# A transformer block on one core: three quarter products of the second MLP product split again into seven, weight sums made in DRAM by adding transfers

## The chip, the core and the metric

The program runs on one core of one Trainium2 chip. The metric is the device time of one execution in microseconds; lower is better. The kernel before was run three times: 1228.98, 1229.09 and 1229.5 us, median 1229.09 us. One more execution was recorded by the profiler and gives the trace that is read here. The engines are PE (TensorE: matmuls, with PEld for its weight loads), DVE (VectorE), ACT (ScalarE), POOL (GpSimd) and SP (SyncE, which issues most of the DMAs here; ACT and POOL issue DMAs from queues of their own).

## The reference

One layer of a hybrid encoder, 1024 tokens by 1024 channels, float32. What matters here is the order of the stages and the last two lines:

```python
h = rms(x, norm1_g[l]).astype(dt)
p = h @ w_in[l]
...
mix_a = mlstm_group(qk_m, ...)
mix_b = diff_attention_group(...)
mixed = jnp.concatenate([mix_a, mix_b], axis=-1).astype(dt)
x = x + (mixed @ w_out[l]).astype(dt)
u = rms(x, norm2_g[l]).astype(dt) @ w_ff1[l]
u = jnp.square(jax.nn.relu(u))
x = x + (u @ w_ff2[l]).astype(dt)
```

`w_ff1` is 1024 x 4096 and `w_ff2` 4096 x 1024. `mlstm_group` has 4 heads of 128 with a forward and a backward scan over 8 chunks of 128 tokens, `diff_attention_group` 4 heads over blocks of 128 queries. The last line, `u @ w_ff2`, is the second MLP product.

## The kernel before

The program goes through its stages one after the other: start and projections, mLSTM (about 134 to 340 us), attention (340 to 565), the output projection and the second norm (to 612), the first MLP product (612 to 917) and the second (917 to 1223).

**Precision.** Each float32 operand is cut into a high part (ACT, `cut_hi`, L1736) and a low part (DVE, `cut_lo`, L1739). A product of tiles is three matmuls into one PSUM bank: high by high, low by high, high by low (for the second MLP product lines L2152, L2153, L2154).

**Quarter products.** Both MLP products are done by the Strassen-Winograd scheme: the matrices are halved both ways, and seven products of halves, numbered 1 to 7, take the place of eight; sums of halves are made before, and sums of products after. The first MLP product writes, for each of the seven, the token side that the second needs to DRAM (`g_dram`, seven times eight tiles of 128 x 1024). Its last steps are the sums `sums1`, `sums2`, `sums3` of a pair of tiles and the stores of these.

**The second MLP product** (L2066 to L2240) has seven products in the order 1, 6, 2, 5, 7, 3, 4, each of 8 steps. A step (`z_step`, L2136) takes one tile of weights (`wa`: `wa0h`, `wa0l`, `wa1h`, `wa1l`) and one of tokens (`wb`, `we`: `wbh`, `wbl`, `weh`, `wel`), and has 24 matmuls of 128 x 128 weights by 128 x 512 tokens. Both kinds of cut tiles have two buffers, which the steps use by turns. The sums of weight halves are made by DVE on the raw weights: `za+zs` (L2115), `za-zd` (L2112), `zs+zd` (L2226), `zt+za` (L2116), eight of each. `finish` (L2183) recombines the products, on DVE, ACT and a little on POOL, with the residual, and stores the output. The last step's output tile is done in two halves of 256 columns, stored from ACT's and SP's queues (`last_out`, L2169).

**Order.** Instructions of each engine run in the order in which they stand in its program. That order comes from tables: `when(t, f, ...)` puts a piece of work at a planned time `t`, and the pieces are emitted in order of `t`. In the MLP the unit of `t` is half a step of the second product (2.725 us by the plan), and `T2` is where the second product begins. In the mLSTM stage a heap of the same kind is emptied while the projection's matmuls are emitted, with `clock` as its time. DMAs on SP's queue can also come out in another order than they were emitted, by what each waits for.

**The mLSTM stage** interleaves two streams on PE: projections (`pj_c`, `pva`) and the heads. For each head and each half `g` of the chunks, `load(g)` (L1102) loads two broadcast tiles of 512 KB, `e` from `m_dram` (decays) and `qs` from `sc_dram` (scales); head 0's are called e00, qs00, e01 and qs01 in what follows. `select` (L1116, POOL) masks `e`; `exps` (L219, ACT) exponentiates it; `scores` (L1177, DVE) multiplies it by the scores; `scaled` (L1181, DVE) multiplies `qs` by `q`; `sums` (L1194 and L1196, PE, tile `tot`) uses both. Then `divide`, `squares`, `unit` and `turned` (L1209, L180, L1224, L1230) normalise and turn the head's output; of these POOL has the tensor operations with `to` and `nd`. POOL also makes the low parts of the projection's weights (L1028: `w_c`, `w_va`). In the attention stage POOL has small operations, most of them on `sm` (L1435).

Of the kernel before, what the change touches and what calls it, by code (L numbers as in the profile page):

```python
# [10 lines left out]
F32 = mybir.dt.float32  # L11
# [129 lines left out]
def hybrid_block_kernel(ctx: ExitStack, tc: tile.TileContext, xT, xR, w_v, w_k, w_c, w_va, w_qg, w_o, w_1, w_2, vec, rel, outT):  # L141
# [20 lines left out]


# [1480 lines left out]

    gate_pieces()
# [138 lines left out]
    for j in range(4):  # L1784
# [147 lines left out]
    for c in range(N_PAIR):  # L1932
# [17 lines left out]
        when(e[4] + 0.28, sums1, c)  # L1950
        when(e[4] + 0.8, sums2, c)
        when(e[4] + 1.3 if c + 1 < N_FIRST else e[4] + 1.4, sums3, c)
        for d, i, f in ((0.9, 7, lambda c: gs1[c][:, 0]), (0.95, 5, lambda c: gs1[c][:, 1]),
                        (1.3, 6, lambda c: gs2[c][:, 0]), (1.9, 4, lambda c: gs2[c][:, 1])):
            when(e[4] + d, lambda c, i, f: store(i, c, f(c)), c, i, f)
# [139 lines left out]
    def load_za(j):
        za[j] = z_load(z_tile(f"za{j}", f"za{j}", pool="a"), j, 0, 0)

    def load_zs(j):
        zs[j] = z_load(z_tile(f"zs{j}", f"zs{j}"), j, 1, 0)

    def load_zd(j):
        zd[j] = z_load(z_tile(f"zd{j}", f"zd{j}"), j, 1, 1)

    def load_zt(i, j):
        zt[i, j] = z_load(z_tile(f"zt{i}_{j}", "zt", 3), j, 0, 1)

    def z_add(t, a, b):
        nc.vector.tensor_tensor(t[0], a[0], b[0], op=add)

    def z_seven(j):  # L2110
        zt[7, j] = z_tile(f"zt7_{j}", "zt", 3)
        nc.vector.tensor_tensor(zt[7, j], za[j], zd[j], op=sub)  # L2112

    zsum = {
        6: lambda j: nc.vector.tensor_tensor(za[j], za[j], zs[j], op=add),  # L2115
        3: lambda j: nc.vector.tensor_tensor(zt[3, j], zt[3, j], za[j], op=add),  # L2116
        7: z_seven,
    }
    zsrc = {1: lambda j: za[j], 6: lambda j: za[j], 5: lambda j: zs[j], 4: lambda j: zd[j]}
    graw = {}  # L2120

    def fetch(s):
        i, j = steps[s]
        graw[s] = ypool.tile([P, 2, HB], F32, tag=f"y0_{(s + 1) % 4}", name=f"g{i}_{j}")
        nc.sync.dma_start(graw[s], g_dram[i - 1][j].rearrange("c p t -> p c t"))

    def g_part(s):
        return (wb, we)[s % 2], graw[s]

    def z_part(s):  # L2130
        i, j = steps[s]
        return wa[s % 2], zsrc[i](j) if i in zsrc else zt[i, j]
# [194 lines left out]
```

## Time and profile before

| what | value |
|---|---|
| median of three runs | 1229.09 us |
| the profiled execution | 1229.11 us |
| its span (first to last instruction) | 1227.3 us |
| bytes moved by DMA | 218.04 MB, mean 178 GB/s |
| mLSTM, 134 to 340 us | the longest waits of PE: 0.8, 0.4, 0.3 and 0.3 us in all |
| the second product's first and last matmul | 917.5 and 1222.6 us |

The page is of one execution. "Busy" is the time in which an engine had an instruction; matmuls overlap, so the duration of one is longer than the distance between two. A row such as `PE tot L1194 <- DVE e L1177` says that PE, at the instruction that writes tile `tot`, waited for the instruction of L1177 that wrote `e` on DVE, and then for how long in all, how often, and the longest. In a timeline a bracket behind a row gives the idle time of the engine before it and what ended it. For a DMA, the engine's name with q means the queue that issued it, and the landing time is counted from the issue.

### The profile page before, as it was taken

What the parts mean: (1) busy time and instruction counts of PE and PEld (TensorE: products, weight loads), DVE (VectorE), ACT (ScalarE), POOL (GpSimd) and SP (SyncE); (2) the same over time, 40 slices, a digit from 0 to 9 for tenths busy, and PEclk for the clock granted to TensorE, in tenths of its full rate; (3) what the DMA queues carried; (4) which work ended last, traced back from release to release, by engine and by line L of the source; (5) the groups of instructions that cost most, each with busy time, mean ns of one, the idle gap of its engine ahead of it and who ended that gap; (6) DMA issues with size and microseconds to landing.
All of it is one profiled execution on the core that took longest, in us unless ns stands there. A gap on an engine that the chain in (4) does not pass through costs nothing.

```text
span 1227.3 us, 17165 instructions
## 1 busy us (share of the span) xinstructions
PE 1217.3 (99%) x6349; PEld 1020.7 (83%) x6349; DVE 848.1 (69%) x1202; ACT 651.2 (53%) x1158; POOL 242.7 (20%) x271
## 2 busy tenths in 40 slices
PE   9999999999999999999999999999999999999998
PEld 8889888888878878888887888888888888888886
DVE  7885668983277787674789886666754864558754
ACT  7785457676356676664465455454453433333332
POOL 2135323662344453321000000000000000014001
PEclk9999999999999999999999999999999999999999
DMA  9972665344364685517445764444369655435632
GB/s 284 237 242 105 214 137 135 98 139 131 129 199 161 209 281 171 169 61 267 161 152 195 252 217 128 155 160 140 137 217 377 214 188 188 145 121 164 222 115 92
DMA packets 106024, 218.04 MB, mean 178 GB/s; under 512 B 9424, under 2 KB 22224, under 8 KB 105936
## 3 DMA queue, kind: packets, MB, share of 16 engines
q1 hardware_dynamic: 84276, 168.27, 42.2%
q0 software_dynamic: 9856, 27.30, 7.6%
q10 hardware_dynamic: 11808, 21.37, 4.7%
q8 instruction: 50, 0.82, 0.3%
q14 instruction: 34, 0.28, 0.1%
HBM read 157.56 MB, written 58.30 MB: 176 GB/s over the span
## 4 chain that ended last, share of the span: by engine, by line
PE 86%; DVE 5%; DMA 4%; ACT 2%; issue 2%; POOL 1%; ACTq 0%; SPq 0%; DVEq 0%; POOLq 0%
PE z L2154 8%; PE z L2152 8%; PE z L2153 8%; PE m L1823 7%; PE m L1824 7%; PE m L1825 7%; PE pav L1426 4%; PE pva L1296 4%; PE pl L1386 3%; PE pv L435 3%; PE pvz L435 3%; PE pw L229 3%; PE pw L231 2%; PE pw L230 2%; PE pa L1414 2%
## 5 line engine op out<-in xcount | busy, mean ns | idle before, releaser
L2197 POOL TENSOR_TENSOR zx<-zx,res 128x512 f32<-128x512 f32 x4 | 8.7, 2179 | 491.6 <-DVE zx L2195 491.6
L1391 DVE CUSTOM_DVE_ANT_0 l<-pl,toe 128x1024 f32<-128x1024 f32 x64 | 76.3, 1221 | 17.0 <-PE pl L1386 15.9
L2154 PE MATMUL z<-wbh,wa0l 128*128 128x512 f32 x224 | 87.4, 390 | 0.1
L2153 PE MATMUL z<-wbl,wa0h 128*128 128x512 f32 x224 | 87.2, 389 | 0.0
L2154 PE MATMUL z<-weh,wa1l 128*128 128x512 f32 x224 | 87.2, 389 | 0.0
L2153 PE MATMUL z<-wel,wa1h 128*128 128x512 f32 x224 | 87.2, 389 | 0.0
L2152 PE MATMUL z<-wbh,wa0h 128*128 128x512 f32 x224 | 87.2, 389 | 0.0
L2152 PE MATMUL z<-weh,wa1h 128*128 128x512 f32 x224 | 87.2, 389 | 0.0
L1736 ACT ACTIVATE wbh<-g 128x1024 fp32r<-128x1024 f32 x28 | 29.7, 1061 | 90.2 <-PE z L2154 53.0
L1736 ACT ACTIVATE weh<-g 128x1024 fp32r<-128x1024 f32 x28 | 29.7, 1061 | 90.2 <-PE z L2154 53.4
L1739 DVE TENSOR_TENSOR wel<-g,weh 128x1024 fp32r<-128x1024 f32 x28 | 35.2, 1258 | 56.6 <-ACT weh L1736 56.6
L1872 ACT ACTIVATE sq<-sq 128x512 f32<-128x512 f32 x48 | 30.2, 630 | 82.3 <-DVE sq L1911 65.7
L1397 ACT ACTIVATE l<-l,sm 128x1024 f32<-128x1024 f32 x64 | 73.1, 1148 | 0.5 <-DVE sm L1391 0.5
L1739 DVE TENSOR_TENSOR wbl<-g,wbh 128x1024 fp32r<-128x1024 f32 x28 | 35.4, 1264 | 52.4 <-ACT wbh L1736 52.4
L1426 PEld LDWEIGHTS pav<-v,at 128*128 128x128 f32 x512 | 61.5, 192 | 3.4 <-issue 1.1
L1426 PE MATMUL pav<-v,at 128*128 128x128 f32 x512 | 62.7, 276 | 0.0
L1386 PE MATMUL pl<-kk,q 64*128 64x512 f32 x384 | 55.6, 410 | 1.1 <-DVE sm L1391 1.0
L229 PE MATMUL pj_c<-hhi,w_c 128*128 128x512 f32 x128 | 53.4, 417 | 0.0
L229 PE MATMUL pw<-mix,hi_wo 128*128 128x512 f32 x128 | 52.1, 407 | 0.0
L231 PE MATMUL pj_c<-hhi,w_c 128*128 128x512 f32 x128 | 50.3, 393 | 0.0
L231 PE MATMUL pw<-mix,lo_wo 128*128 128x512 f32 x128 | 50.1, 391 | 0.0
L2154 PEld LDWEIGHTS z<-wbh,wa0l 128*128 128x128 f32 x224 | 42.0, 188 | 9.6 <-DVE wa0l L1739 0.9
(507 smaller groups left out, 3610.8 us busy)
## 6 DMA issues: line engine op xcount, KB each, us to landing
g<-g_dram SPq DMA_DIRECT2D x56, 512.0 KB, 3.7
g_dram<-gs SPq DMA_DIRECT2D x64, 256.0 KB, 3.5
g_dram<-sq ACTq DMA_DIRECT2D x42, 256.0 KB, 2.7
kk<-k_dram POOLq DMA_DIRECT2D x16, 512.0 KB, 6.2
raw_wo<-in_w_o_dram SPq DMA_DIRECT2D x16, 512.0 KB, 3.6
re<-in_w_dram SPq DMA_DIRECT2D x16, 512.0 KB, 4.3
ro<-in_w_dram SPq DMA_DIRECT2D x16, 512.0 KB, 3.7
zt<-in_w_dram SPq DMA_DIRECT2D x16, 512.0 KB, 4.0
```

The lines of the kernel that those rows point to most:

```text
L229: nc.tensor.matmul(out, ahi, bhi, start=start, stop=False)
L231: latest[0] = nc.tensor.matmul(out, alo, bhi, start=False, stop=stop).ins
L435: latest[0] = nc.tensor.matmul(o, x[:, tt], y, start=start and j == 0 and n == 0, stop=stop and j == 3 and n == 2, skip_group_check=True,).ins
L1386: nc.tensor.matmul(it.pl[x][:, sl], hd.q[r, i, qi * P : (qi + 1) * P], hd.kk[r, j, sl], start=n == 0, stop=n == 2)
L1391: nc.vector.tensor_tensor_reduce(lt, it.pl[m], hd.toe[:, off : off + S], 1.0, 3.0e38, ALU.add, ALU.min, it.sm[:, m : m + 1])
L1426: nc.tensor.matmul(it.pav[:, 0:P], at, it.head.v[:, c], start=c == 0, stop=c == NC - 1)
L1823: nc.tensor.matmul(p, wh, xh, start=go, stop=False, skip_group_check=True)
L1824: nc.tensor.matmul(p, wh, xl, start=False, stop=False, skip_group_check=True)
L1825: nc.tensor.matmul(p, wl, xh, start=False, stop=stop and k == 3, skip_group_check=True)
L2152: nc.tensor.matmul(p, wh, gh, start=go, stop=False, skip_group_check=True)
L2153: nc.tensor.matmul(p, wh, gl, start=False, stop=False, skip_group_check=True)
L2154: nc.tensor.matmul(p, wl, gh, start=False, stop=end, skip_group_check=True)
```

## The change

Products 1, 2 and 4 of the second MLP product are each halved both ways again and done as seven products of quarter size. A quarter product has two fine steps (q = 0, 1), each with 24 matmuls of 128 x 128 weights by 128 x 256 tokens (four contraction blocks, two output halves, three parts). So three times seven times two, 42 fine steps, take the place of 24 coarse ones; products 6, 7, 5 and 3 stay as they are, 32 steps. Fine steps of 1, 2 and 4 are interleaved with coarse ones of 6, 7 and 5, two fine and one coarse in turn, and product 3 stands last. Cut tiles have three buffers. The tokens of a fine product stay in SBUF in two wide tiles, in which DVE makes the token sums of the inner scheme (`wide_sum`, 24 in all).

DVE makes no weight sums any more. All sums of weights, of the outer scheme (tiles `s5`, `s6`, `s7`, eight each) and of the inner ones (`so` with the product's and the inner product's number and q), are made in DRAM: a transfer copies one tile, and a second transfer, issued by POOL, adds another to it. There are 48 copies and 56 adds of 512 KB: in the mLSTM stage 28 copies from ACT's queue and 12 adds from POOL's; in the attention stage 16 adds; in the first MLP product 14 copies from SP and 14 adds; in the second 6 copies and 14 adds. The weights of a step are then one plain load of a tile from the inputs `w_2`, `w_2q` or from a sum. There are 74 such loads, 32 of token tiles and 24 into the wide tiles, where there were 40 of weights and 56 of tokens before.

The core of the diff:

```diff
+    s7 = [tc.dram_tile([P, 1024], F32, name=f"s7_{j}") for j in range(8)]
+    s6 = [tc.dram_tile([P, 1024], F32, name=f"s6_{j}") for j in range(8)]
+    s5 = [tc.dram_tile([P, 1024], F32, name=f"s5_{j}") for j in range(8)]
+    so = {(i, p): [tc.dram_tile([P, 1024], F32, name=f"so{i}{p}_{q}") for q in range(2)] for i in (1, 2, 4) for p in (5, 6, 7, 3)}
...
+    def copy_in(dst, src):
+        copier[0].dma_start(dst, src)
+
+    def add_to(dst, src):
+        nc.gpsimd.dma_start(dst, src, accum_op=ALU.add, max_dma_last_dim=4096)
...
+    spread(2.0, 3.0, coarse_sums("c5") + fine_sums("c7 c5", 1) + coarse_sums("c7") + fine_sums("c7 c5", 2) + fine_sums("c7 c5", 4), push)
+    spread(22.0, 4.4, coarse_sums("a5") + fine_sums("a7 a5", 1), push)
...
+    slots = (2, 3.5, 6, 7.5, 10, 11.5, 18, 19, 20, 22, 23, 24, 26, 27, 28, 30)
+    for n, ((f, *args), t) in enumerate(zip(coarse_sums("a7") + fine_sums("a7 a5", 2) + fine_sums("a7 a5", 4), slots)):
+        push((t, 10**6 + 200 + n, f, args))
...
-        when(e[4] + 0.28, sums1, c)
-        when(e[4] + 0.8, sums2, c)
-        when(e[4] + 1.3 if c + 1 < N_FIRST else e[4] + 1.4, sums3, c)
+        d = c == N_PAIR - 1
+        when(e[4] + (7.5 if d else 0.28), sums1, c)
+        when(e[4] + (10.5 if d else 0.8), sums2, c)
+        when(e[4] + (14 if d else 1.3 if c + 1 < N_FIRST else 1.4), sums3, c)
...
-    steps = [(i, j) for i in (1, 6, 2, 5, 7, 3, 4) for j in range(NJ)]
+    P_ORDER = (1, 2, 5, 6, 7, 3, 4)
+    U2 = 1.035
+    steps = []
+    for two, one in ((1, 6), (2, 7), (4, 5)):
+        fine = [[(two, p, q) for q in range(2)] for p in P_ORDER]
+        coarse = [(one, 0, j) for j in range(NJ)]
+        if one == 6:
+            steps += [coarse.pop(0)]
+        for g in fine:
+            steps += g + coarse[:1]
+            coarse = coarse[1:]
+        steps += coarse
+    steps += [(3, 0, j) for j in range(NJ)]
...
+    pairs(44.2, 4.2, [fine_sums(x, 1) + coarse_sums(x) + fine_sums(x, 2) + fine_sums(x, 4) for x in ("c6", "a6")])
+    pairs(T2 + 6.2, 4.0, [fine_sums(x, 1) + fine_sums(x, 2) for x in ("c3", "a3")])
+    pairs(T2 + 34.2, 4.0, [fine_sums(x, 4) for x in ("c3", "a3")])
...
+    def wide_sum(i, p, q):
+        b11, b12, b21, b22 = (quarter(i, q, *x) for x in ((0, 0), (0, 1), (1, 0), (1, 1)))
+        out, x, y, op = {5: (b11, b11, b12, sub), 6: (b11, b22, b11, add), 7: (b12, b22, b12, sub), 4: (b11, b11, b21, sub)}[p]
+        nc.vector.tensor_tensor(out, x, y, op=op)
...
-    zsum = {
-        6: lambda j: nc.vector.tensor_tensor(za[j], za[j], zs[j], op=add),
-        3: lambda j: nc.vector.tensor_tensor(zt[3, j], zt[3, j], za[j], op=add),
-        7: z_seven,
-    }
...
+    def fine_step(s):
...
+        for j in range(4):
+            for n in range(2):
+                o = banks[x][:, n * 256 : (n + 1) * 256]
...
+                nc.tensor.matmul(o, wh[:, j, nn], gh[:, j], start=go, stop=False, skip_group_check=True)
+                nc.tensor.matmul(o, wh[:, j, nn], gl[:, j], start=False, stop=False, skip_group_check=True)
+                nc.tensor.matmul(o, wl[:, j, nn], gh[:, j], start=False, stop=end, skip_group_check=True)
...
+    def add_after(s, f, *args):
+        nc.gpsimd.tensor_copy(pace, graw[s][:, 0, 0:1])
+        f(*args)
...
+    for j, x in enumerate(coarse_sums("a3")):
+        when(step_at[place[5, 0, j]] - 6, add_after, place[5, 0, j], *x)
```

How this moves instructions, at three places.

SP at the beginning of the mLSTM stage, with the first loads of head 0 (`qs` and `e`, numbered by head and half; line numbers of the changed program are 51 higher there). Before:

```order
L921 DMA dec_dram_62<-ends_1856 64x1
L1102 DMA qs00_1954<-sc_dram_61 128x2x512
L934 DMA decb_188<-dec_dram_62 128x64
L1102 DMA e00_1953<-m_dram_60 128x2x512
L1102 DMA qs01_2017<-sc_dram_61 128x2x512
L1020 DMA raw_c6_2039<-in_w_c_dram 128x1024
L1102 DMA e01_2016<-m_dram_60 128x2x512
```

And SP at the same place in the changed program:

```order
L972 DMA dec_dram_62<-ends_1906 64x1
L1153 DMA qs00_2007<-sc_dram_61 128x2x512
L985 DMA decb_236<-dec_dram_62 128x64
L1153 DMA qs01_2071<-sc_dram_61 128x2x512
L1153 DMA e00_2006<-m_dram_60 128x2x512
L1071 DMA raw_c6_2093<-in_w_c_dram 128x1024
L1153 DMA e01_2070<-m_dram_60 128x2x512
```

The load of qs01 has moved ahead of that of e00; the rest stands as it was.

POOL in the changed program, from head 1's second `e` to head 0's normalised output, with adds into `s5`:

```order
L1167 AFFINE_SELECT e10_2314<-e10_2314 128x512 x2
L1260 TENSOR_TENSOR to01_2269<-to01_2269,nd01_2329 128x4x128
L189 DMA s5_2_195<-in_w_2_dram 128x1024
L1167 AFFINE_SELECT e11_2387<-e11_2387 128x512 x2
L1146 MEMSET va2_2420 128x8
L189 DMA s5_3_196<-in_w_2_dram 128x1024
L1079 TENSOR_TENSOR w_c3_2228<-raw_c3_2227,w_c3_2228 128x1024
L231 TENSOR_TENSOR nd00_2300<-nd00_2300,mhalf_235 128x4
L1275 TENSOR_TENSOR to00_2245<-to00_2245,nd00_2300 128x4x128
```

Without the two rows of L189 these are the rows before the change: one add now stands ahead of the select of e11, one behind it, ahead of `w_c3`, `nd00` and `to00`.

POOL in the changed program again, some 40 us later, from head 2's second `e` to the last weights of `pva`:

```order
L1167 AFFINE_SELECT e21_2752<-e21_2752 128x512 x2
L1079 TENSOR_TENSOR w_va1_2563<-raw_va1_2562,w_va1_2563 128x1024
L231 TENSOR_TENSOR nd11_2681<-nd11_2681,mhalf_235 128x4
L1275 TENSOR_TENSOR to11_2620<-to11_2620,nd11_2681 128x4x128
L189 DMA s5_7_200<-in_w_2_dram 128x1024
L1079 TENSOR_TENSOR w_va2_2702<-raw_va2_2701,w_va2_2702 128x1024
L189 DMA so17_0_205<-in_w_2q_dram 128x1024
L1079 TENSOR_TENSOR w_va3_2799<-raw_va3_2798,w_va3_2799 128x1024
L189 DMA so17_1_206<-in_w_2q_dram 128x1024
```

Here too only the rows of L189 are new: one add ahead of `w_va2`, one between it and `w_va3`, one behind.

On PE, DVE and ACT nothing moves ahead of the second MLP product, apart from the 28 copies among ACT's instructions in the mLSTM stage.

More of the change, by code (lines that the diff above doesn't have):

```diff
@@ L140, in hybrid_block_kernel @@
 @with_exitstack
[L141 removed]
+def hybrid_block_kernel(ctx: ExitStack, tc: tile.TileContext, xT, xR, w_v, w_k, w_c, w_va, w_qg, w_o, w_1, w_2, w_2q, vec, rel, outT):
     nc = tc.nc
@@ L2077, in open_za @@
         zpools["a"] = mctx2.enter_context(tc.tile_pool(reuse_waits="tile", name="zapool", bufs=1, side="right"))
+        wide[1] = [zpools["a"].tile([P, 4, 2, HB], F32, tag=f"A{q}", name=f"wide1{q}") for q in range(2)]
     def open_z():
@@ L2081, in open_z, with add_row, pairs @@
         zpools["z"] = ctx.enter_context(tc.tile_pool(reuse_waits="tile", name="zpool", bufs=1))
+        zp["w"].append(parts(zpools["z"], "zw", [P, 2, HB]))
+        zp["g"].append(parts(zpools["z"], "zg", [P, 2, HB]))
+    def add_row(x):
+        table.append(x)
+    copier[0] = nc.sync
+    def pairs(first, each, what):
+        for n, (copy, more) in enumerate(zip(*what)):
+            for x, d in ((copy, -2.6), (more, 0)):
+                table.append((first + each * n + d, 10**6 + len(table), x[0], x[1:]))
@@ L2095, in load_za @@
[L2095 to L2112, printed above, removed]
```

330 lines of the change are left out of this document (235 added, 95 removed), and 2 rows, old and new, of the table moved.

## The prediction

> **What bounds the kernel now.** I read the page's busy line first, then busy time by stage, then the second product's matmuls and their waits.
>
> ```profile
> span 1227.3 us, 17165 instructions
> ...
> PE 1217.3 (99%) x6349; PEld 1020.7 (83%) x6349; DVE 848.1 (69%) x1202; ACT 651.2 (53%) x1158; POOL 242.7 (20%) x271
> ```
>
> ```profile
> 170.00:205.00 35.00, 34.72 (x208) 30.41 (x207) 26.07 (x33) 23.66 (x54) 10.36 (x8) 1.00 0.54 135
> 205.00:240.00 35.00, 34.88 (x214) 30.66 (x213) 30.08 (x39) 26.31 (x71) 17.11 (x14) 1.00 0.42 117
> 240.00:275.00 35.00, 34.62 (x207) 29.92 (x207) 31.46 (x40) 26.28 (x72) 23.14 (x15) 1.00 0.48 146
> ...
> 446.00:565.00 119.00, 118.79 (x790) 99.84 (x789) 82.30 (x146) 73.25 (x148) 41.37 (x69) 1.00 0.47 154
> ...
> 612.00:917.00 305.00, 303.87 (x1342) 250.42 (x1342) 225.28 (x310) 152.31 (x229) 1.92 (x1) 1.00 0.52 176
> 917.00:1223.00 306.00, 305.82 (x1347) 252.32 (x1346) 191.48 (x172) 114.89 (x118) 23.08 (x12) 1.00 0.54 182
> ```
>
> Behind the stretch stand its length and the busy time of PE, PEld, DVE, ACT and POOL, then granted clock (1.00 throughout), DMA share, GB/s. PE is busy 99% of the span and nearly all of every stage, so the time is the sum of PE's work plus whatever makes PE wait. Taking matmuls away in the last stage shortens the kernel by their whole time, and any new PE wait anywhere, 700 us earlier too, is added in full.
>
> ```profile
> L2152 PE MATMUL z<-wbh,wa0h x224: 387/389/396, 917.5 to 1216.7; 128*128 128x512 f32 x112
> ...
> L2154 PE MATMUL z<-weh,wa1l x224: 388/389/402, 923.9 to 1222.6; 128*128 128x512 f32 x112
> ```
>
> ```profile
> PEld z L2154 <- DVE wa0l L1739: 0.9, 2, 0.6
> ```
>
> The second product is 7 products x 8 steps x 24 matmuls = 1344. They start from 917.5 to 1222.6: 305.1 us for 1343 intervals, 227 ns each (the 389 ns of one overlap), **5.45 us a step**. Their only stall is 0.9 us at the beginning.
>
> **What goes and what comes on PE.** Products 1, 2 and 4 lose 3 x 8 = 24 steps: 24 x 5.45 = 130.8 us. In their place come 3 x 7 x 2 = 42 fine steps of 24 matmuls of 256 columns. Such matmuls stand in the projections, in triples that alternate with triples of 272.
>
> ```profile
> 82.55 0.28 PE L229 MATMUL pqa<-w_qa,hhi 128*128 128x256 f32 x1
> ...
> 82.89 0.28 PE L229 MATMUL pqa<-w_qa,hhi 128*128 128x272 f32 x1
> ...
> 83.26 0.28 PE L229 MATMUL pqa<-w_qa,hhi 128*128 128x256 f32 x1
> ...
> 87.61 0.28 PE L229 MATMUL pqa<-w_qa,hhi 128*128 128x256 f32 x1
> ```
>
> ```profile
> 400.29 1.94 PE L1426 MATMUL pav<-v,at 128*128 128x128 f32 x16
> 402.07 1.04 PE L1414 MATMUL pa<-ident,l 128*128 128x128 f32 x8
> ```
>
> From 82.55 to 87.61 are seven pairs of triples: 5.06 / 42 = 120.5 ns a matmul. The first triple of 256 takes 0.34 us (113 ns), that of 272 0.37 us (123 ns). Scaling 120.5 by 256/264 gives 117; I take **117.5 ns**. Bounds: from below the 128-column matmuls, 16 in 1.78 us, 111 ns each, with the same loads of 128 weight columns; from above 125 ns, the 272 ones rounded up. A fine step then takes 24 x 117.5 = 2.82 us, 42 take 118.4 us (111.9 to 126.0). **PE: 118.4 - 130.8 = -12.4 us** (-18.9 to -4.8). Half a coarse step would be 2.725 us: the seven-for-eight saving is 16.4 us, of which 4 us go to narrower matmuls.
>
> A rule speaks for a larger gain. The Trainium skill, "TensorE: Matmul & The Clock Gate", section "Back-to-back issue gap", gives N/2.4 + 2.5 ns, 109 ns at 256 columns. An estimate by it is 42 x 24 x 109 = 109.9 us and -20.9 us; the 117 ns of the rows disagree, and the measurement decides.
>
> **DVE and ACT in the second product.**
>
> ```profile
> L1739 DVE TENSOR_TENSOR wel<-g,weh 128x1024 fp32r<-128x1024 f32 x28 | 35.2, 1258 | 56.6 <-ACT weh L1736 56.6
> ...
> L2112 DVE TENSOR_TENSOR zt<-za,zd 128x1024 f32<-128x1024 f32 x8 | 10.9, 1356 | 0.0
> L2115 DVE TENSOR_TENSOR za<-za,zs 128x1024 f32<-128x1024 f32 x8 | 9.8, 1225 | 0.3
> ...
> L2226 DVE TENSOR_TENSOR zs<-zs,zd 128x1024 f32<-128x1024 f32 x8 | 9.7, 1218 | 0.0
> ...
> L2116 DVE TENSOR_TENSOR zt<-zt,za 128x1024 f32<-128x1024 f32 x8 | 9.7, 1218 | 0.0
> ...
> L2190 DVE TENSOR_TENSOR zv<-z,zx 128x512 f32<-128x512 f32 x4 | 2.7, 682 | 0.0
> ```
>
> The 32 weight sums go to DMA: 10.9 + 9.8 + 9.7 + 9.7 = 40.1 us of DVE, which cost the end nothing since DVE was busy 191.5 of 306. There are 74 steps for 56, so 36 more low cuts (45.3 us), 24 sums over the wide tiles (24 x 1.22 = 29.3) and, for 23 recombinations of about 0.68 (16), 40 of that size and 8 of twice it (37). DVE: 191.5 - 40.1 - 16 + 45.3 + 29.3 + 37 = 247 of 294 us, 84%. In a phase of 14 fine and 8 coarse steps (14 x 2.82 + 8 x 5.45 = 83 us) stand 44 cuts, 8 wide sums and some 10 recombinations: 55 + 10 + 7 = 72 us, 87%. With three buffers a coarse step's cuts have two fine steps, 5.64 us, and need four of 1.26 us at most behind ACT's: about a microsecond spare. I take 0.5 us of stalls in the stage (0 to 5). The 36 more high cuts on ACT fit into its idle 190 us. At the beginning the last pair's sums and stores stand later and the first cuts earlier, so I take 0.6 of the 0.9 us as gained (-0.9 to +1). The tail behind the last matmul keeps its form (two halves on two queues): nothing either way, since the same last step of product 3 for 4 and the same two stores follow.
>
> **The transfers.** 48 copies and 56 adds of 512 KB come in, and no step of the trace shows either between DRAM tiles. The nearest rows are the start's accumulating transfers.
>
> ```profile
> 28.68 0.87 POOL L335 DMA_DIRECT2D raw_k<-xtv  x1 [4.31 <-DVE w_t L368]
> ```
>
> ```profile
> q1 hardware_dynamic: 5186, 10.94, 51.7%
> q0 software_dynamic: 1440, 4.19, 39.0%
> ```
>
> Both queue rows are of 0 to 60 us. Plain transfers (q1) took 0.517 x 60 / 10.94 = 2.8 us of all 16 engines per MB, 1.5 us per 512 KB. The POOL queue, most of it accumulating, took 0.390 x 60 / 4.19 = 5.6, so 2.9 us. An add holds POOL 0.87 us to issue.
>
> *First product (14 copies and 14 adds)*: 14 x 4.4 = 62 us over 305 raise the DMA share from 0.52 to 0.72, and POOL had one instruction there: 0. *Second product*: 34 more loads, 6 copies and 14 adds, 34 x 1.5 + 6 x 1.5 + 14 x 2.9 = 101 us on 165, over 294 us a share of 0.90; loads are issued some 17 us ahead, which covers it (inside the 0.5 above). SP's copies there read sums that were added a stage earlier. POOL's eight adds into s6 wait for product 5's tiles; behind them POOL has only more adds, and product 3's loads, which need them, come up to a phase later. *Attention (16 adds)*:
>
> ```profile
> POOL sm L1435 <- ACT on L1431: 91.3, 28, 5.0
> ```
>
> POOL waits 91.3 us, so 0.87 us of issue hides before nearly each `sm`: 0.3 us (0 to 2).
>
> **mLSTM (28 copies from ACT, 12 adds from POOL)** is where I lose time: PE's slack is nil at three places.
>
> (1) *The order on SP*. Before, head 0's first decay tile e00 was loaded ahead of the second scale tile qs01; now qs01 goes first.
>
> ```profile
> 169.80 0.38 SPq L1102 DMA_DIRECT2D e<-m_dram  x1
> 170.27 0.42 SPq L1102 DMA_DIRECT2D qs<-sc_dram  x1
> ```
>
> ```profile
> e<-m_dram SPq DMA_DIRECT2D x1, 512.0 KB, 10.8
> qs<-sc_dram SPq DMA_DIRECT2D x1, 512.0 KB, 14.4
> ```
>
> ```profile
> 182.14 1.28 ACT L219 ACTIVATE e<-e,ucol 128x128 f32<-128x128 f32 x4 [2.09 <-POOL e L1116]
> ```
>
> ```profile
> 185.81 1.23 DVE L1181 TENSOR_TENSOR qs<-q,qs 128x1024 f32<-128x1024 f32 x1 [3.49 <-ACT q L219]
> ...
> 199.33 1.22 DVE L1177 TENSOR_TENSOR e<-ps,e 128x1024 f32<-128x1024 f32 x1
> ```
>
> ```profile
> PE tot L1194 <- DVE e L1177: 0.3, 1, 0.3
> ```
>
> e00 landed at 180.6 and qs01 at 184.7, one behind the other; exchanged, e00 lands about 4.1 us later. POOL's select waits for it, ACT's exponentials for that (2.09 us idle), `q` is queued behind them on ACT, and DVE waits for `q` (3.49). From 185.81 DVE has no gap until the tile e01 at 199.33, for which PE waits 0.3 us. So all **4.1 us** reach PE (0 to 5.6: the upper end has one copy, 1.5 us, in the way).
>
> (2) *POOL's issues.*
>
> ```profile
> 213.86 2.20 POOL L1116 TENSOR_SCALAR_AFFINE_SELECT e<-e 128x512 f32<-128x512 f32 x2 [4.94 <-DMA e<-m_dram]
> ...
> 251.28 3.04 POOL L1116 TENSOR_SCALAR_AFFINE_SELECT e<-e 128x512 f32<-128x512 f32 x2 [2.04 <-DMA e<-m_dram]
> ...
> 259.88 5.73 POOL L1028 TENSOR_TENSOR w_va<-raw_va,w_va 128x1024 fp32r<-128x1024 f32 x2
> ```
>
> ```profile
> PEld pva L1296 <- POOL w_va L1028: 0.3, 1, 0.3
> PEld po L1230 <- POOL to L1224: 0.3, 1, 0.3
> ```
>
> From each select POOL runs without a gap to the tile for which PE waits: `to` (head 1), `w_va` (ready at 265.6). The add into s5_3 stands in the first run, those into s5_7 and so17_0 in the second: 3 x 0.87 = **2.6 us** (0 to 2.6). The other nine stand where POOL waits.
>
> (3) *Later loads.* Both selects wait for their e tile to land, so its delay goes straight on. 28 copies and 12 adds are 42 + 35 = 77 us of engine time in 206, on shares of 0.42 to 0.54. One copy beside each load, half of it in the way: 2 x 0.7 = **1.4 us** (0, to 2 x 4.4 with a copy and an add in the way).
>
> Sum here +8.1 us (0 to 17).
>
> **The sum.** -12.4 - 0.6 + 0.5 + 0 + 0.3 + 8.1 = -4.1 us. From the profiled execution's 1229.11 (span 1227.3 and 1.8 around it), 0.02 us over the median of the runs, that is **1225.0 us**.
>
> **The rivals.**
> - *The loads are not late* (chance 0.22). If qs01 and e00 share the engines rather than follow each other, and the issues slip into POOL's waits, mLSTM loses 0 to 3: 1217 to 1220, about 1218. For it: the DMA share is 0.54 there, and POOL idles 4.94 and 2.04 us before the two runs. Against: 180.6 and 184.7 are one load apart.
> - *The e tiles are late by whole transfers* (0.15), the slower side. It is contention in mLSTM: with 4.1 + 1.5 for e00, 4.4 each for the two others and 2.6 of issues, 17 us go there: 1229.1 - 12.9 + 0.8 + 17 = 1234. It decides from 12.1 us lost, where the gain is eaten. For it: PE has no slack at these places. Against: SP's loads are few.
> - *DVE becomes the bound of the fine phases* (0.05). From 1.26 x 83 / 72 = 1.45 us an operation, DVE is the longer engine; at 1.6, with 52 of them and 7 us, a phase takes 90 us for 83: 1225 + 7 for each phase it strikes, 1232 with one.
> - *Narrow matmuls at 111 ns* (0.05): 6.5 us more gained, 1218.5. For it: the 128-column rows; against: 113 to 117 for 256. The skill's rule above would point to this side.
> - *They cost 125 ns or more* (0.03), so that seven for eight hardly saves: 7.6 us less gained, 1232.6; from 130 ns (130.8 / 1008) the split saves nothing.
>
> **How the numbers follow.** My forecast has 0.50, from 1220 to 1230 by itself. Such a kernel's measurement tells about 0.2%, 2.5 us, from no change: faster is below 1226.6, slower above 1231.6. Faster: 0.33 of the forecast's chance, 0.22 and 0.05, together 0.60. Same: the other 0.17 of the forecast and 0.03 of the rivals, 0.20. Slower: 0.20. The range that leaves out two in ten, reaching to both the first and the second rival, is 1215 to 1235.
>
> **What would show it.** In the second product: 42 fine steps of 2.82 us between the first and last z matmul, 293 us in all, and PE's waits there under 1 us. In mLSTM: PE waiting some 4 us for `e` at about 200 us, the e00 select near 185, POOL's runs longer by 0.87 and 1.7 us, and the attention stage beginning some 8 us later. I am wrong on the sign of a term if the first product starts no later than before, and on the price of the split if a fine step is not 2.7 to 3.0 us.

## The result, and the profile after

| | median, us | lowest to highest, runs |
|---|---|---|
| before | 1229.03 | 1228.73 to 1229.5, 4 |
| after | 1245.32 | 1242.94 to 1246.89, 4 |

The ratio is 1.0131, with a 95% interval of 1.0113 to 1.0148: the change made the kernel slower by 16 us, where 4 us less had been forecast. The profiled execution of the changed kernel took 1246.89 us. Its page begins:

```profile
span 1245.1 us, 18390 instructions
...
PE 1215.9 (98%) x6781; PEld 1038.0 (83%) x6781; DVE 889.9 (71%) x1253; ACT 693.1 (56%) x1200; POOL 267.4 (21%) x323
...
q1 hardware_dynamic: 84692, 196.58, 46.4%
q0 software_dynamic: 17920, 56.66, 21.1%
q10 hardware_dynamic: 12704, 36.05, 8.0%
```

PE works less than before (1215.9 for 1217.3 us), and the span is 17.8 us longer: PE waits. q1 is SP's queue, q10 ACT's, q0 POOL's. The adds show their price here. The kernel before had 27.30 MB on q0, at 7.6% of its span. What the change puts on top took (0.211 x 1245.1 - 0.076 x 1227.3) / (56.66 - 27.30) = 5.8 us of all 16 engines per MB, 3.0 us for an add of 512 KB. The same difference on q10 gives 2.9 us per MB, 1.5 us for a copy. Both prices are those of the prediction (2.9 and 1.5 us).

Busy time by stretch, columns as before (length; PE, PEld, DVE, ACT, POOL; granted clock, DMA share, GB/s):

```profile
170.00:205.00 35.00, 32.93 (x180) 28.16 (x179) 22.80 (x28) 22.01 (x50) 10.95 (x9) 0.95 0.80 227
205.00:240.00 35.00, 26.34 (x145) 22.99 (x144) 19.56 (x30) 18.15 (x59) 15.05 (x15) 0.86 0.81 193
240.00:275.00 35.00, 34.61 (x205) 30.01 (x205) 27.23 (x34) 22.75 (x60) 14.11 (x12) 0.99 0.77 212
275.00:310.00 35.00, 29.01 (x168) 24.70 (x167) 20.67 (x30) 22.35 (x63) 18.83 (x16) 0.95 0.89 234
...
446.00:565.00 119.00, 117.96 (x810) 97.77 (x809) 90.57 (x163) 80.47 (x163) 60.36 (x90) 1.00 0.80 227
...
612.00:917.00 305.00, 303.09 (x1340) 249.47 (x1339) 233.46 (x318) 152.21 (x224) 13.41 (x15) 1.00 0.72 218
```

The DMA share between 170 and 275 us was 0.42 to 0.54 before and is 0.77 to 0.81 now, with 0.89 behind it. PE has holes, and behind them the granted clock, 1.00 everywhere before, is as low as 0.86. What PE waited for between 134 and 340 us (the longest four):

```profile
PE po L1281 <- POOL to L1275: 8.7, 1, 8.7
PE pd L1200 <- DVE st L1209: 3.4, 2, 2.0
PE pva L1352 <- ACT w_va L270: 2.7, 1, 2.7
PE pva L1352 <- POOL w_va L1079: 1.9, 1, 1.9
```

Behind the longest of these stands POOL, in its timeline:

```profile
227.39 2.20 POOL L1167 TENSOR_SCALAR_AFFINE_SELECT e<-e 128x512 f32<-128x512 f32 x2 [13.71 <-DMA e<-m_dram]
...
232.45 1.33 POOL L231 TENSOR_TENSOR nd<-nd,mhalf 128x4 f32<-128x4 f32 x1
233.85 1.04 POOL L1275 TENSOR_TENSOR to<-to,nd 128x512 f32<-128x512 f32 x1
```

The select of e11 (head 1, second half) waits 13.71 us for its load, where it waited 4.94; `w_c`, `nd` and `to` are queued behind it, and PE needs `to`. And behind the second longest is DVE's wait for the decays `decb`, a load of 32 KB, 6.7 us where it was 3.3 in the kernel before:

```profile
DVE st L1209 <- DMA decb<-dec_dram: 6.7, 1, 6.7
```

The second product did become shorter. Its first and last matmuls:

```profile
L2261 PE MATMUL z<-weh,wa0h x144: 389/389/397, 943.6 to 1234.7; 128*128 128x512 f32 x144
...
L2263 PE MATMUL z<-wbh,wa1l x88: 388/389/389, 1108.4 to 1240.6; 128*128 128x512 f32 x88
```

From 943.6 to 1240.6 are 297.0 us, for 305.1 before: 8.1 us gained. It began 26.1 us later.

**Lateness.** The order of PE's instructions is the same in both kernels up to the second product. So each matmul of the one can be set against the same matmul of the other, and the difference of their start times (the median over 8 us of the kernel before) says where time goes. This table has it for all kernels that follow too; the columns are times of the kernel before.

| us late at | 165 | 195 | 232 | 300 | 600 | 900 |
|---|---|---|---|---|---|---|
| after | 0.6 | 4.2 | 15.0 | 23.6 | 25.0 | 26.1 |
| f1: copies alone | 0.2 | 6.1 | 8.6 | 11.7 | 12.7 | 13.9 |
| f2: adds alone | 6.5 | 6.7 | 6.5 | 10.3 | 9.9 | 10.4 |
| g3: both | 0.6 | 7.0 | 17.5 | 25.5 | 26.1 | 26.4 |
| g1: both, 32 KB each | 0.6 | 1.3 | 1.2 | 5.8 | 5.9 | 5.8 |
| e8: the later 21 copies | 0.5 | 0.3 | 4.4 | 6.6 | 6.9 | 6.9 |
| e4: copies in 4 KB rows | 0.6 | 6.1 | 15.2 | 22.2 | 27.4 | 27.7 |
| e5: transfers moved | 0.9 | 0.7 | 0.5 | 0.5 | 0.7 | 15.2 |
| e6: moved otherwise | 0.8 | 1.2 | 1.2 | 1.3 | 15.0 | 15.2 |
| e7: moved once more | 0.8 | 0.5 | 0.1 | 0.2 | 1.5 | 1.3 |

For the changed kernel: 3.6 us at 179 to 195, 10.9 at 222 to 232, 8.6 at 260 to 270, then 1.4 in the attention stage and 1.1 in the first product. 23.0 us are lost in mLSTM.

### The profile page after: what moved, and what is told of

Read it like the earlier page. It is cut to its first block, busy times and chain, and to the rows that moved or that the text cites. A ratio compares the mean times of both kernels' runs of the same rounds, so it can differ in the third digit from the quotient of the medians.

```text
span 1245.1 us, 18390 instructions
## 1 busy us (share of the span) xinstructions
PE 1215.9 (98%) x6781; PEld 1038.0 (83%) x6781; DVE 889.9 (71%) x1253; ACT 693.1 (56%) x1200; POOL 267.4 (21%) x323
## 3 DMA queue, kind: packets, MB, share of 16 engines
q0 software_dynamic: 17920, 56.66, 21.1%
## 4 chain that ended last, share of the span: by engine, by line
PE 81%; DMA 7%; DVE 5%; issue 3%; POOL 2%; ACT 2%; SPq 0%; ACTq 0%; DVEq 0%; POOLq 0%
PE m L1882 7%; PE m L1883 7%; PE m L1884 7%; PE z L2261 5%; PE z L2262 5%; PE z L2263 5%; PE pav L1482 4%; PE pl L1442 3%; PE pva L1352 3%; PE z L2282 3%; PE z L2281 3%; PE z L2280 3%; PE pvz L486 3%; PE pw L280 3%; PE pw L282 2%
## 5 line engine op out<-in xcount | busy, mean ns | idle before, releaser
L1447 DVE CUSTOM_DVE_ANT_0 l<-pl,toe 128x1024 f32<-128x1024 f32 x64 | 76.3, 1221 | 16.1 <-PE pl L1442 15.4
L189 POOL DMA_DIRECT2D so<-in_w_2q_dram x24 | 21.2, 884 | 307.5 <-DMA so<-so 307.1
L2263 PE MATMUL z<-weh,wa0l 128*128 128x512 f32 x144 | 56.1, 390 | 0.2 <-DVE wa0l L1798 0.2
L2261 PE MATMUL z<-weh,wa0h 128*128 128x512 f32 x144 | 56.2, 390 | 0.0
L2262 PE MATMUL z<-wel,wa0h 128*128 128x512 f32 x144 | 56.2, 390 | 0.0
L280 PE MATMUL pw<-mix,hi_wo 128*128 128x512 f32 x128 | 52.0, 406 | 0.0
L281 PE MATMUL pj_c<-hlo,w_c 128*128 128x512 f32 x128 | 51.3, 401 | 0.0
L281 PE MATMUL pw<-mix,hi_wo 128*128 128x512 f32 x128 | 49.9, 390 | 0.0
L1352 PE MATMUL pva<-w_va,hhi 128*128 128x512 f32 x128 | 44.9, 412 | 4.5 <-ACT w_va L270 2.7
L2282 PE MATMUL z<-zgh,zwl 128*128 128x256 f32 x168 | 47.6, 284 | 0.8 <-DVE zwl L1798 0.8
L2280 PE MATMUL z<-zgh,zwh 128*128 128x256 f32 x168 | 47.6, 283 | 0.1
L2281 PE MATMUL z<-zgl,zwh 128*128 128x256 f32 x168 | 47.5, 283 | 0.0
L1442 PEld LDWEIGHTS pl<-kk,q 64*128 64x128 f32 x384 | 34.8, 184 | 15.1 <-DVE sm L1447 4.2
L189 POOL DMA_DIRECT2D s<-in_w_dram x32 | 27.0, 855 | 90.3 <-DMA s<-s 75.7
```

What stands on the lines that cost most here:

```text
L280: nc.tensor.matmul(out, ahi, bhi, start=start, stop=False)
L281: nc.tensor.matmul(out, ahi, blo, start=False, stop=False)
L1442: nc.tensor.matmul(it.pl[x][:, sl], hd.q[r, i, qi * P : (qi + 1) * P], hd.kk[r, j, sl], start=n == 0, stop=n == 2)
L2261: nc.tensor.matmul(p, wh, gh, start=go, stop=False, skip_group_check=True)
L2262: nc.tensor.matmul(p, wh, gl, start=False, stop=False, skip_group_check=True)
L2263: nc.tensor.matmul(p, wl, gh, start=False, stop=end, skip_group_check=True)
```

## The experiments

The theory after the result (A): the copies and adds take the DMA engines from the few loads of the mLSTM stage that PE's chain waits for. Its rivals: the adds alone do it (B); the exchange of qs01 and e00 in SP's order (C, the prediction's); the copies' large rows (D); issues and queues, not bytes (E).

**Copies alone, on the kernel before.** ACT issues 28 copies at the change's times:

```diff
+    for n in range(28):
+        heapq.heappush(table, (2.0 + 3.0 * n, 10**6 + 100 + n, nc.scalar.dma_start, (spare[n], w_2[n])))
```

> The kernel before with the 28 copies of 512 KB issued from ACT's queue in the mLSTM stage, at the planned times of the change, into tiles that nobody reads; no adds, and the second product as before. Theory A (the copies' share of the DMA engines delays the small loads of the stage): the copies are in flight through the whole stage, the scale decay load (decb) lands some 10 us after its issue, PE loses about 4 us at 180 us and 5 to 8 us more by the two late e tiles: 1238 to 1241 us. Theory B (the adds do it, with nearly twice the engine time each and from POOL's own queue): only the first 4 us, 1231 to 1234 us. Theory C (the exchange of qs01 and e00 in SP's order costs 4.1 us by itself, as the prediction had it): a wait of PE for e at about 200 us.

One execution: 1242.39 us (before, on that chip, 1229.81). 11.4 us are lost in mLSTM. PE's waits there:

```profile
PE po L1231 <- POOL to L1225: 2.8, 1, 2.8
PE pd L1150 <- DVE st L1159: 2.6, 1, 2.6
PE pva L1299 <- ACT w_va L220: 2.4, 1, 2.4
PE ps L1176 <- ACT q L220: 1.2, 1, 1.2
```

They stand at the places of the change, but shorter. The loads of `e` took

```profile
DMA to landing us min/median/max: 11.5/13.6/17.1
```

where they took 7.9/10.0/11.2 before. Theory A's losses came, a little larger than expected; B falls. SP's order is the exchanged one in this kernel too, and PE does not wait for `e` at 200 us. But PE is 6 us late there already, so this alone does not decide about C.

**Adds alone, on the kernel before.** POOL issues 12 adds at the change's times:

```diff
+    for n in range(4):
+        heapq.heappush(table, (0.5 + 0.1 * n, 10**6 + 100 + n, nc.sync.dma_start, (spare[n], w_2[n])))
+    for n in range(12):
+        heapq.heappush(table, (22.0 + 4.4 * n, 10**6 + 200 + n, add_to, (spare[n % 4], w_2[n])))
```

> The kernel before with the 12 adds from POOL's queue in the mLSTM stage, at the planned times of the change, into four tiles that nobody reads (filled by four plain copies from SP's queue when the stage begins); no other copies. Theory A: the engine time of the adds alone is 35 us of 206, and one add lies beside each of the late e tiles: PE loses 2.6 us by POOL's issues and 1 to 3 us at each tile, 1234 to 1238 us. Theory B: most of the 24 us lost ahead of the attention stage, 1243 to 1249 us. If only POOL's issue time counted: 1231.7 us.

One execution: 1239.03 us. At 300 us PE is 10.3 us late, but 6.5 of them are lost already in the start stage, and by the experiment itself. The four plain copies that fill the tiles were meant for the beginning of the mLSTM stage. They wait for nothing, and SP issued them at 19.2 us:

```profile
19.22 3.26 SPq L730 DMA_DIRECT2D spare<-in_w_dram  x4
```

The loads of `raw_k`, issued by POOL just behind them, then took a median of 11.5 us, for 6.4 before, and ACT and PE waited:

```profile
30.97 0.63 ACT L352 ACTIVATE w_t<-raw_k 128x512 fp32r<-128x512 f32 x1 [6.21 <-DMA raw_k<-in_w_v_dram]
```

So here copies delay a load on PE's chain at another place. What the adds cost in mLSTM is the difference, 3.8 us, all of it between 260 and 270 us:

```profile
PE pva L1304 <- POOL w_va L1029: 1.9, 1, 1.9
PE pva L1304 <- ACT w_va L220: 1.3, 1, 1.3
```

The loads of `e` took 10.2/10.7/12.3 us. e11's 10.2 us, for 9.2 before, are not enough to reach PE at 222. e21's are the 12.3, for 7.9 before, and POOL's select of it begins 4.4 us later than PE's lateness accounts for. From this select to the end of the last `w_va` POOL took 13.7 us, for 14.3 before. So these 3.8 us came with a late load and not with the issues in POOL's run. They are a little less than theory A expected (2.6 us by issues and 1 to 3 at each tile).

**Both, but small, on the kernel before.** The 28 copies and 12 adds with 8 of 128 rows each; SP's order is the exchanged one:

```diff
-        heapq.heappush(table, (2.0 + 3.0 * n, 10**6 + 100 + n, nc.scalar.dma_start, (spare[n], w_2[n])))
+        heapq.heappush(table, (2.0 + 3.0 * n, 10**6 + 100 + n, nc.scalar.dma_start, (spare[n][0:8], w_2[n][0:8])))
+    for n in range(12):
+        heapq.heappush(table, (22.0 + 4.4 * n, 10**6 + 200 + n, add_to, (spare[n][0:8], w_2[n + 12][0:8])))
```

> The kernel before with the 28 copies and 12 adds of the mLSTM stage at their places and on their queues, but each of 8 rows (32 KB) in the place of 512 KB; their results are read by nobody. SP's order is the exchanged one (qs01 ahead of e00). Theory A (engine time of the transfers): nothing to lose but POOL's issues, PE reaches the attention stage less than 3 us late, 1229 to 1232 us. Theory C (the exchange in SP's order costs 4.1 us by itself): 4 us late, with PE waiting for e at about 200 us. Theory E (issues, and waits of ACT's and POOL's queues for earlier transfers): 10 us late or more.

One execution: 1234.39 us (before 1230.53); 5.2 us lost, where theory A had expected less than 3. Of these 0.8 are lost between 165 and 195 us, and 4.6 by 270 us, nearly all of them at 260 to 270, for POOL's `w_va`:

```profile
PE pva L1304 <- POOL w_va L1029: 2.4, 2, 1.9
...
PE tot L1195 <- DVE e L1178: 0.2, 1, 0.2
```

This parts three things. *C is out as a price of 4.1 us*: with the exchanged order PE waits 0.2 us for `e`, as before (0.3). e00 was selected at 182.6 us, for 180.8 before, and not 4.1 us later: the first loads don't follow each other as whole transfers. DVE came to the tile e01 1.2 us later. *E is small*: from the end of `to` to the end of the last `w_va`, with two issues among them, POOL took 6.3 us, for 5.7 before (6.4 in the changed kernel). Of the 4.6 us, 1.5 came with e21, which landed after 9.4 us for 7.9, 1.3 with a longer run of POOL from the select on, the issues included, and some 1.5 with the granted clock, which was 0.50 from 272 to 274 us. Why e21 was later among so small transfers stays open. *The rest, some 18 us of the change, needs the bytes*: `e` lands in 8.3/9.4/10.2 us when the transfers are small.

**Both, of full size, on the kernel before.**

```diff
-        heapq.heappush(table, (2.0 + 3.0 * n, 10**6 + 100 + n, nc.scalar.dma_start, (spare[n][0:8], w_2[n][0:8])))
+        heapq.heappush(table, (2.0 + 3.0 * n, 10**6 + 100 + n, nc.scalar.dma_start, (spare[n], w_2[n])))
...
-        heapq.heappush(table, (22.0 + 4.4 * n, 10**6 + 200 + n, add_to, (spare[n][0:8], w_2[n + 12][0:8])))
+        heapq.heappush(table, (22.0 + 4.4 * n, 10**6 + 200 + n, add_to, (spare[n], w_2[n + 12])))
```

> The kernel before with both the 28 copies and the 12 adds of 512 KB in the mLSTM stage, read by nobody, and the second product as before. Copies alone made PE 12.2 us late at the attention stage and adds alone 4.1 us. Theory A with three queues sharing the engines: the load of e11 and that of e21 get about a third of the engines while a copy and an add are both in flight, so the two losses are more than their sum: 22 to 25 us late as in the changed kernel, 1252 to 1255 us. If the losses simply add: 16 us late, 1246 us.

One execution: 1254.94 us; 24.9 us lost in mLSTM. So the 40 transfers alone, without the new second product, make the change's loss. PE's waits:

```profile
PE po L1231 <- POOL to L1225: 8.5, 1, 8.5
PE pd L1150 <- DVE st L1159: 6.3, 3, 3.2
PE pva L1304 <- ACT w_va L220: 2.6, 1, 2.6
```

and `e` landed in 9.6/16.9/18.5 us. The losses do not add: 11.4 and 3.8 apart are 15.2, together they are 24.9. At 222 us the adds alone cost nothing, the copies 2.5, both 10.5. Much of this is in the landing of e11 already: 9.2 us before, 10.2 with adds, 13.6 with copies, 18.5 with both, so delays of 1.0 and 4.4 us apart and of 9.3 together. (e21's nearly add: 4.4 and 3.6 us apart, 9.0 together.) The changed kernel's DMA queues while e11 was on its way show what happens (217 to 227.3 us; packets, MB, share of the 16 engines):

```profile
q10 hardware_dynamic: 87, 1.31, 33.5%
q1 hardware_dynamic: 978, 0.70, 31.0%
q0 software_dynamic: 142, 0.52, 29.5%
```

Three queues have work, and each has nearly a third of the engines' time. SP's queue, with the load that everybody waits for, got 31%. e11 landed after 18.7 us for 9.2. The packets themselves were slower by less than half: one of 2 KB on SP's queue took 0.14 us on average between 205 and 214 us in the kernel before, and 0.18 us (208 to 217) and 0.20 us (217 to 227) here. So the load mostly lacked turns. The Trainium skill says it in general ("DMA: Bandwidth & Descriptors", section "Issuing engines are not separate DMA queues"): transfers issued by different engines run on the same 16 DMA engines and interleave. These rows agree, and show the shares.

**Copies in smaller rows, in the changed kernel.**

```diff
-        copier[0].dma_start(dst, src)
+        copier[0].dma_start(dst, src, max_dma_last_dim=4096)
```

> The changed kernel with its copies cut into rows of 4 KB (128 by 1024 elements) where they had rows of 32 KB (16 by 8192); all else the same. Theory D (a copy's 32 KB rows hold an engine for about a microsecond at a time, and the loads' 2 KB packets take turns with them one for one): the e tiles land several us earlier, and the time drops by 8 us or more, below 1237 us. Theory A (what counts is the sum of engine time): no change beyond 3 us, 1242 to 1248 us.

ACT's queue had 300 packets for 1.10 MB between 217 and 227 us, where it had 87 for 1.31. One execution: 1248.76 us, just above the 1242 to 1248 of theory A; 21.6 us lost in mLSTM for 23.0. Theory D is out: the size of a copy's rows hardly matters here. In the attention stage this execution lost 5 us, the changed kernel 1.4; why stays open.

**Later copies only, on the kernel before.**

```diff
-    for n in range(28):
+    for n in range(7, 28):
```

> The kernel before with the last 21 of the 28 copies alone in the mLSTM stage (the first seven, issued up to some 190 us, are left out); read by nobody. With all 28, PE lost 5.8 us by 189 us (its wait for decb's users among it), 2.8 at 222 and 2.9 at 263. Theory A (each loss belongs to the load that the copies in flight delay): the first 5.8 us are gone and the others stay, PE 5 to 7 us late at the attention stage, 1234 to 1237 us. If a copy's time is lost wherever it falls: three quarters of 12.2, 9 us late, 1239 us.

One execution: 1235.36 us. The loss up to 195 us (5.9 with all copies) is gone; at 222 us 4.1 are lost, at 265 us 2.2. Each loss belongs to the load that is on its way while copies are. At 222 us PE waited

```profile
PE po L1231 <- POOL to L1225: 3.2, 1, 3.2
```

and became 4.1 us late: the clock, 0.50 at 226 to 228 us, makes the difference (see the last section).

**The transfers moved, three ways.** If A is right, the second product's 8 us can be kept by moving the 28 copies and 12 adds to where no load is urgent. First: 16 copies to the attention stage, 12 pairs into the first third of the first product.

```diff
-    spread(2.0, 3.0, coarse_sums("c5") + fine_sums("c7 c5", 1) + coarse_sums("c7") + fine_sums("c7 c5", 2) + fine_sums("c7 c5", 4), push)
-    spread(22.0, 4.4, coarse_sums("a5") + fine_sums("a7 a5", 1), push)
...
+    copies = coarse_sums("c7") + fine_sums("c7 c5", 2) + fine_sums("c7 c5", 4)
+    for n, ((_, *args), t) in enumerate(zip(copies, slots)):
+        push((max(0.2, t - 1.8), 10**6 + 300 + n, nc.sync.dma_start, args))
...
+    pairs(3.0, 3.4, [fine_sums(f"{x}7 {x}5", 1) + coarse_sums(f"{x}5") for x in "ca"])
     pairs(44.2, 4.2, [fine_sums(x, 1) + coarse_sums(x) + fine_sums(x, 2) + fine_sums(x, 4) for x in ("c6", "a6")])
```

> The changed kernel with nothing added in the mLSTM stage: 16 of its 28 copies are issued by SP in the attention stage, ahead of the adds that need them, and the other 12 copies with the 12 adds go into the first third of the first MLP product. All theories by which the transfers of the mLSTM stage cost the 24 us: PE reaches the attention stage as early as before, the second product still gains 8 us, and 1 to 4 us go in the first MLP product, where the DMA share rises towards 1: 1222 to 1225 us. If the loss is rather in the number of bytes of the whole program, wherever they are: 1235 us or more.

1233.14 us (10 runs, 1229.52 to 1237.18; the profiled one 1236.73), ratio to before 1.0029 (1.0014 to 1.0045). In the profiled execution mLSTM and attention lose nothing, SP's order of e00 and qs01 is the old one again, and 14.5 us go in the first product, between 640 and 740 us:

```profile
DVE v L1962 <- DMA x_b<-x_dram: 11.5, 4, 6.2
PE m L1883 <- DVE w L1966: 10.0, 4, 4.1
```

That is the part in which spilled tiles are loaded again just in time. DVE waited 11.5 us for those from `x_dram`, for 3.0 before, and PE for DVE: the same fault at another place. The expectation of 1 to 4 us there was wrong. Second: nothing ahead of unit 44 of the first product, 17 pairs behind it, 3 pairs at the end of attention, and 6 behind mLSTM's last e tile.

```diff
+    early = [fine_sums(f"{x}7 {x}5", 1) + coarse_sums(f"{x}5") for x in "ca"]
+    for n in range(6):
+        for k in range(2):
+            f, *args = early[k][n]
+            push((72.0 + 3.0 * n + 4.0 * k, 10**6 + 100 + n, f if k else nc.scalar.dma_start, args))
...
-    pairs(3.0, 3.4, [fine_sums(f"{x}7 {x}5", 1) + coarse_sums(f"{x}5") for x in "ca"])
-    pairs(44.2, 4.2, [fine_sums(x, 1) + coarse_sums(x) + fine_sums(x, 2) + fine_sums(x, 4) for x in ("c6", "a6")])
+    pairs(44.2, 3.5, [fine_sums(f"{x}6", 1) + coarse_sums(f"{x}6") + fine_sums(f"{x}6", 2) + fine_sums(f"{x}6", 4) + coarse_sums(f"{x}5")[5:] for x in "ca"])
```

> The changed kernel with its transfers away from the loads that PE waits for: 6 copies (ACT) and 6 adds behind the last e tile of the mLSTM stage, 16 copies (SP) and 16 adds in the attention stage, 3 pairs at its end, and 17 pairs in the first MLP product, all behind its first 44 units, in which the spilled tiles are loaded again. Theory A: nothing lost in mLSTM and attention, 1 to 3 us in the first MLP product, 8 gained in the second: 1221 to 1225 us. If any place costs as much as the time that its transfers take on the engines, 1232 us or more.

1236.1 us (5 runs, 1234.5 to 1237.63), ratio 1.0043 (1.0029 to 1.0057), and not the 1221 to 1225 us expected. The first product loses 0.2 us with 17 pairs, but 13.7 go where attention begins:

```profile
326.26 0.89 POOL L189 DMA_DIRECT2D so<-in_w_2q_dram  x1 [3.50 <-DMA so<-in_w_2q_dram]
...
331.94 1.46 POOL L1423 DMA_DIRECT2D kk<-k_dram  x2
```

In POOL's timeline the loads of the first attention keys `kk` stand behind the adds, each of which waits there for its copy to land. They were issued at 331.9 us for 321.7 before and took a median of 14.6 us to land for 8.7, and PE waited 7.8 us for them. Third: nothing in mLSTM, 20 copies and 20 adds in attention, 3 pairs at its end, 19 pairs behind unit 44.

```diff
-    for n in range(6):
-        for k in range(2):
-            f, *args = early[k][n]
-            push((72.0 + 3.0 * n + 4.0 * k, 10**6 + 100 + n, f if k else nc.scalar.dma_start, args))
...
+    for n, t in enumerate((17, 21, 25, 29)):
+        for k in range(2):
+            f, *args = early[k][n]
+            push((t - 1.8 * (1 - k), 10**6 + 500 + n, f if k else nc.sync.dma_start, args))
...
-    pairs(44.2, 3.5, [fine_sums(f"{x}6", 1) + coarse_sums(f"{x}6") + fine_sums(f"{x}6", 2) + fine_sums(f"{x}6", 4) + coarse_sums(f"{x}5")[5:] for x in "ca"])
+    pairs(44.2, 3.2, [fine_sums(f"{x}6", 1) + coarse_sums(f"{x}6") + fine_sums(f"{x}6", 2) + fine_sums(f"{x}6", 4) + coarse_sums(f"{x}5")[3:] for x in "ca"])
```

> The changed kernel with no transfer at all in the mLSTM stage: 20 copies (SP) and 20 adds in the attention stage, 3 pairs at its end and 19 pairs in the first MLP product behind its first 44 units. Places that cost nothing in the two kernels before this: the attention stage with 16 and 16 (DMA share up to 0.97), its end with 3 pairs, and the later part of the first MLP product with 17 pairs. Theory A: PE reaches the second product at most 2 us late, and the 8 us there are kept: 1221 to 1225 us, faster than both kernels. If the engines' time is now the limit in the attention stage or in the first MLP product: 1226 to 1232 us.

**1221.44 us** (5 runs, 1219.47 to 1222.08; before 1229.53), ratio 0.9932 (0.9918 to 0.9945): faster than both kernels. By stretch:

```profile
134.00:340.00 206.00, 204.42 (x1160) 174.36 (x1159) 138.44 (x208) 125.57 (x318) 80.12 (x70) 1.00 0.51 140
...
446.00:565.00 119.00, 118.43 (x794) 99.67 (x793) 82.06 (x146) 74.27 (x151) 57.66 (x88) 1.00 0.97 291
...
612.00:917.00 305.00, 303.87 (x1345) 250.72 (x1344) 223.97 (x309) 152.14 (x228) 17.37 (x20) 1.00 0.79 242
```

The same transfers are made, and in the attention stage the DMA share of 0.97 costs PE 1.3 us at most. The second product runs from 918.8 to 1215.9 us, 297.1 us, as in the changed kernel.

## Why the prediction was wrong

1. **What bounds the kernel: right.** PE is the bound, and a new wait 700 us ahead of the change's own stage was added in full.
2. **The split: right in sign, too large.** -12.4 us were forecast for PE and -12.5 for the stage with its stalls; -8.1 came. The interval of the fine matmuls is the first reason:

```profile
1000.04 0.28 PE L2280 MATMUL z<-zgh,zwh 128*128 128x256 f32 x1
1000.16 0.28 PE L2281 MATMUL z<-zgl,zwh 128*128 128x256 f32 x1
...
1001.24 0.28 PE L2281 MATMUL z<-zgl,zwh 128*128 128x256 f32 x1
```

   Ten intervals in 1.20 us, 120 ns for the 117.5 that I took: 1008 x 2.5 = 2.5 us. I had scaled the mean of 256 and 272 columns (120.5) by the width; the mean unscaled was the better number. The second reason is the stage's beginning, where PE's weight loads waited 1.9 us in all and not 0.3:

```profile
PEld z L2282 <- DVE zwl L1798: 1.0, 1, 1.0
PEld z L2263 <- DVE wa0l L1798: 0.6, 1, 0.6
PEld z L2280 <- ACT zwh L1795: 0.3, 1, 0.3
```

   DVE (236 us busy of 297, for 247 of 294 forecast) and the transfers in the stage (share 0.83) cost no wait beyond that: the rival of DVE as the bound didn't come.
3. **SP's order (term 4.1 us): wrong.** The price was read off two landing times as if e00 waited for the whole of qs01; with the same order and small transfers 0.8 us are lost. The sign that was foretold did come, by luck: the e00 select stands at 185.25 us ("near 185"), and DVE comes to e01 at 203.31 us for 199.33. That delay came with the full-size transfers, not with the order. PE shows no wait for it, since it had by then lost 3.6 us to `decb`, for which DVE waited 3.4 us longer. The later 21 copies without the first seven lose nothing here.
4. **POOL's issues (2.6 us): too large.** From the select of e11 to the end of `to` POOL took 7.5 us with an add in the run, for 8.5 before. From `to` to the last `w_va` it took 6.4 us with two issues among them, for 5.7. An issue has a row of 0.8 to 1.1 us there, but the next row of POOL begins 0.6 us after its start, and the rest of the run was not the same length each time. So some 0.7 us can be put down to the issues.
5. **Later loads (1.4 us): the step that failed.** The prediction put "One copy beside each load, half of it in the way" and so 0.7 us for each e tile, from engine time that would fit, with shares of 0.42 to 0.54. The prices of one copy and one add were right; how much of them gets in the way was not. What counts is how the engines' time is divided while a load is on its way. e11 was 9.5 us late by itself, not 0.7; e21 landed after 15.9 us for 7.9. With `decb`, and with the clock behind each wait, this term is at least what the small transfers did not cost: 23.0 - 5.2, about 18 us.
6. **The hidden terms.** Attention lost 1.4 us (0.3 forecast), the first product 1.1 (0).
7. **The rivals.** "The e tiles are late by whole transfers" was the mechanism that came, with a chance of 0.15 and 1234 us. It had the place and the point from which it decides, and priced the delay at one copy and one add in the way, 4.4 us a tile, half of what came.

The sum by what was measured: 0.6 before 165 us, + 23.0 + 1.4 + 1.1 - 8.1 = +18.0 us, where the spans differ by 17.8.

## What to carry to other kernels

A transfer that nobody waits for isn't free when another, on which a chain hangs, is on its way: where three queues had work, the urgent one got a third of the engines' time, and its load took twice as long, though the mean DMA share of 0.42 to 0.54 before had looked half empty. So before adding background traffic, list the loads whose landing ends an idle time of some engine (here POOL's 4.94 and 2.04 us), keep their flight times free, and look for stages in which every load is issued long ahead; those bore a share of 0.97. And a DMA issue that waits for another transfer holds everything behind it on its engine, other loads too. One that waits for nothing can go out far ahead of its place in the plan, as the four copies at 19 us did: read in the trace when it was issued.

## What the runs showed of the hardware

*The clock.* PE's wait of 8.66 us cost 10.9. Around it, in the changed kernel (columns as above):

```profile
205.00:226.00 21.00, 21.00 (x127) 18.43 (x126) 15.53 (x26) 15.86 (x52) 4.79 (x5) 1.00 0.97 227
226.00:235.00 9.00, 0.34 (x4) 0.15 (x2) 3.86 (x3) 1.28 (x4) 7.53 (x8) 0.73 0.61 148
235.00:240.00 5.00, 5.00 (x17) 4.42 (x18) 0.17 (x1) 1.01 (x3) 2.73 (x3) 0.50 0.49 131
```

After the idle stretch PE runs at a granted clock of 0.50 for 5 us, so this wait was paid again by a quarter. Short waits differ. In the kernel with copies alone a wait of 2.8 us at the same place left the clock at 1.00, and one of 2.6 us, at 182 us, brought it to 0.50:

```profile
182.00:184.00 2.00, 1.87 (x6) 1.69 (x7) 1.96 (x3) 0.28 (x1) 0.00 (x0) 0.50 1.04 211
...
232.00:234.00 2.00, 2.00 (x13) 1.74 (x12) 1.31 (x3) 0.85 (x3) 1.92 (x2) 1.00 0.32 125
```

The Trainium skill has it ("TensorE: Matmul & The Clock Gate", section "Why this matters for your kernels"): no idle gaps above about 3 us between bursts of matmuls, or the clock falls to half. The waits of 8.7 us here and of 3.2 us with the later copies agree. The 2.6 us do not, nor do the small transfers' two waits of 0.5 and 1.9 us close together, behind which the clock was 0.50 too. So 3 us is no safe bound here, and what decides below it no run shows. It also means that the forecast had a term missing: a stall of a few us on PE can have a surcharge.

*The narrow matmul.* 24 matmuls of 256 columns take 2.88 us, 24 of 512 take 5.45: half the width is 53% of the time, so seven-for-eight keeps 9.8 us (130.8 - 121.0) of its 16.4.
